# Two blocks' modulations move from the recurrence to the first phase; the recurrence's filler becomes the gates alone, read in halves of rows

## The chip, the core and the metric

The kernel runs on one core of a Trainium2 chip. The metric is the device time of one execution in microseconds (us), as the median of several runs. One further execution was taken by the hardware profiler; all rows below are from that one.

The engines are named as in the profile: PE is TensorE's matmuls, PEld its weight loads, DVE is VectorE, ACT is ScalarE, POOL is GpSimd, and SP is SyncE, which here only issues DMA transfers. Every engine runs its own instructions in the order in which they were written, and waits at one whose inputs or buffers are not ready.

## The reference

Two transformer-like blocks run one after the other on a sequence of 512 latent tokens (width 1024), with 256 context tokens beside them. The parts that matter here are these, of the first block:

```
s_lat = silu(c);  s_ctx = silu(c_ctx)
mod   = s_lat @ w_ada + b_ada             # six rows of 1024: shift, scale, gate, twice
p_l   = modulate(x, norm1_g, mod[0], mod[1]) @ w_in        # p_c: the same of the context
pool_l, q_l, k_l, v_l, rw_l, gate_l = split(p_l)
att   = differential attention of q_l over the keys of context and latent
rwo   = rwkv: a recurrence over all tokens, in both directions, of rw_c and then rw_l
mix   = sum over n of sigmoid(gate_l[n]) * (branch[n] @ w_br[n]),  then @ w_out
x     = x + mod[2] * mix
x     = x + mod[5] * moe(modulate(x, norm2_g, mod[3], mod[4]))
```

The second block has two layers, each with modulations of its own (`ada_w_0`, `ada_w_1`: 1024 x 6144, times the silu of a second pair of vectors). `mod[0]` and `mod[1]` are needed before anything else. `mod[2]` to `mod[5]` are needed only where the branches are merged, and the second block's only behind the experts. The 24 tiles of `gate_l` (three branches of eight 128-wide tiles) are likewise needed only in the merge.

## The kernel before

Almost all values are float32. A product of a weight and an activation is made of three matmuls of rounded halves (`gemm_k`: high by high, high by low, low by high), and a weight tile is read from DRAM, rounded by ACT (`wgh<-wg`, a CAST) and its remainder formed by DVE (`wgl<-wg,wgh`).

`head1` computes `mod[0]`, `mod[1]` and the normed inputs. Then come two stages that this text is about.

**The first phase** (`phase1`, line 738) weaves four streams: `rwkv_inputs` (projections `gp<-..,ww..` and what the recurrence needs, among it the products `lora`, `dg`, `kss`), `attend` (projections `wa`, then scores `S`, transposes `pt`, value products `o`), `pools_gates` (the pooling branch `wo`, `py`) and `rwkv_blocks` (a small inversion on DVE). Their ranks are 0, 0, 2, 0.

**The recurrence** (`rwkv`, line 1384) weaves two lanes of steps (`rwkv_step`: `pc`, `pw`, `py`, rank 0), two streams of units (`rwkv_unit`: `tkp`, `m`, `pg`, `pT`, `pZ`, `pZt`, `pR`, `pf`, ending in the tile `Zl`; rank 1) and fillers of rank 2. There are 24 units, one for each of four channel groups and six blocks of tokens, and a step waits for the `Zl` of its unit. At most three units are ahead of the steps (`AHEAD`). Most matmuls of units and steps stream 128 or 256 columns.

The fillers of the recurrence are two. The first is `ada_steps`: `mod[2]` to `mod[5]` (`w_ada_b`, 64 pieces of 256 KB) and the first of the second block's modulations (`ada_w0`, 96 pieces). Each piece is one float32 matmul `ada<-wada,adas` with 512 columns and 32 output rows, and four of them in a row go to four different quarters of the output:

```
for j in range(4):
    self.mm(p[32 * j:32 * j + 32], z[:, g + j, ...], W[j], start=..., stop=..., skip_group_check=True)
```

The profile shows each of these as two records, so 160 pieces are 320 records. The second filler is `gates`: for each of the 24 tiles, the projection of the latent tokens (`gp<-h1l_hi,wgh` and its two fellows, 512 columns each), then a tanh (`gt`) and a write to DRAM. Its weights come through a `Feed`, which reads `kc` of the eight row blocks at a time (128 KB a read for `kc=2`), `ahead` reads before they are rounded; a read can start only when the buffer `ahead` places back has been rounded.

Which stream comes next is settled when the program is written, by `weave` and an estimate of when things will be ready (`Clock`):

```
low = 2 if self.clock.active() < self.LOW else 0
x = min(ready, key=lambda x: (x[1] < low, *x[1:3])) if ready else min(S, key=lambda x: x[:3])
```

A filler of rank 2 is thus placed where no stream of lower rank is ready by that estimate, and also where the estimate finds TensorE little used. Nothing is decided at run time. SP's reads stand in one queue in the order of writing, those of the next stage behind those of the stage before.

Of the kernel before, what the change touches and what calls it, by code (L numbers as in the profile page):

```python
# [417 lines left out]
class Builder:  # L418
# [288 lines left out]
    def phase1(self, es):  # L707


        nc, D, tc = self.nc, self.D, self.tc  # L710
        dt = lambda n, sh: tc.dram_tile(sh, FT, name=n)
        self.d_ar = dt("rw_ar", [4, 2, 128, 6, 2, 128])
        self.d_bk = dt("rw_bk", [4, 2, 128, 6, 2, 128])
        self.d_inv = dt("rw_inv", [4, 6, 2, 128, 2, 2, 32])
        self.d_vt = dt("rw_vt", [4, 128, 6, 128])
        self.d_bg = dt("rw_bg", [4, 128, 2, NL])
        self.d_q = dt("at_q", [4, 128, NL])
        self.d_k = dt("at_k", [4, 128, NT])
        self.d_v = dt("at_v", [4, 128, 6, 128])
        self.d_g = dt("gates", [3, 8, 128, NL])  # L720
        self.d_br = [dt(n, [4, 128, NL]) for n in ("pooled", "attended", "rw_out")]
        self.fac = self.pool(es, "keep1").tile([128, 4, 2, 6, 2], FT, name="fac")
        with ExitStack() as e:
            hl = self.pool(e, "h1l")
            self.h1l = [hl.tile([128, 8, NL], FR, name=n) for n in ("h1l_hi", "h1l_lo")]
            with ExitStack() as e2:
                hc = self.pool(e2, "h1c")
                self.h1c = [hc.tile([128, 8, NCX], FR, name=n) for n in ("h1c_hi", "h1c_lo")]
                with ExitStack() as e3:
                    self.banks = dict(g=4, s=4)  # L730
                    self.psp = self.pool(e3, "psh", 1, space=PSUM)
                    self.head1(e3)
                self.banks = dict(g=3, f=2, s=2, h=1)
                self.psp = self.pool(e2, "ps0", 1, space=PSUM)
                self.lat, self.both = [(*self.h1l, 0, NL)], [(*self.h1c, 0, NCX), (*self.h1l, 0, NL)]
                with ExitStack() as e3, ExitStack() as e4:
                    self.todo = []
                    self.weave(*zip(self.RANKS, (self.rwkv_inputs(e3), self.attend(), self.pools_gates(e4), self.rwkv_blocks())))
            self.banks = dict(s=6, g=1, h=1)
            self.psp = self.pool(e, "ps2", 1, space=PSUM)  # L740
            self.rwkv(e)

# [31 lines left out]
    def pools_gates(self, es):  # L774
        with ExitStack() as e:
            yield from self.pool_mixer(e)
        if self.GATES_A:
            yield from self.gates(es, range(self.GATES_A), "h", 3, 4, side="right")

    def gates(self, es, which, tag, ahead, kc, **k):  # L780

        nc = self.nc
        ring = self.pool(es, "gring", **k)
        wp = self.pool(es, "gate", **k)
        at = [(i // 8, i % 8) for i in which]
        feed = self.feed_in(ring, "g", [f"g{b}{n}" for b, n in at], ahead, kc)
        for b, n in at:
            (o,) = yield from self.proj(feed, self.lat, tag)
            t = wp.tile([128, NL], FT, name="gt", tag="gt")
            nc.scalar.activation(t, o, AF.Tanh, scale=0.5)  # L790
            nc.scalar.dma_start(self.d_g[b, n], t)
            yield self.after(t)
# [591 lines left out]
    def rwkv(self, es):  # L1384
        nc = self.nc
        pp = self.pool(es, "rwc", 1)
        up = self.pool(es, "rwu", 1)
        made, done = [0], [0]
        self.levels = pp.tile([128, 3, 2, 128], FT, name="levels")
        nc.scalar.dma_start(self.levels, self.D["levels"])  # L1390

        todo = [(c + q, n) for c in range(0, 4, self.LANES) for n in range(6) for q in range(self.LANES)]
        ch = {}

        def units(q):
            while todo:
                while made[0] - done[0] >= self.AHEAD:
                    yield self.later()
                if todo:
                    c, n = todo.pop(0)  # L1400
                    made[0] += 1
                    P = {}
                    yield from self.rwkv_unit(c, n, up, q, P)
                    ch[c, n] = P

        def steps(q):
            for c in range(q, 4, self.LANES):
                if c == q:
                    while not ch:
                        yield self.later()  # L1410
                V = up.tile([128, 6, 2, 2, 64], FR, name="V", tag=f"V{q}")
                vl = V[:, :, :, 1].bitcast(FT)
                nc.sync.dma_start(vl, self.d_vt[c].rearrange("p j (h v) -> p j h v", h=2))
                nc.scalar.copy(V[:, :, :, 0], vl)
                nc.gpsimd.tensor_sub(V[:, :, :, 1], vl, V[:, :, :, 0].bitcast(FT))
                st = dict(V=V, q=q, y=up.tile([128, 4, 128], FT, name="ysb", tag=f"ysb{q}"), seen=set(), S=None)
                for n in range(6):
                    while (c, n) not in ch:
                        yield self.later()
                    yield from self.rwkv_step(c, n, ch.pop((c, n)), st, up)  # L1420
                    done[0] += 1
                self.dump(f"ysb{c}", st["y"])
                yield from self.rwkv_out(c, st["y"], pp)

        gens = [(0, steps(q)) for q in range(self.LANES)] + [(1, units(q)) for q in range(self.UNITS)]
        self.weave(*gens, (2, self.ada_steps(self.pool(es, "adaw"), self.ada_jobs())),
                   (2, self.gates(es, range(self.GATES_A, 24), "g", 1, 2)))
        nc.vector.tensor_add(self.mod1[:, 16:], self.mod1[:, 16:], self.v("b_ada", 16, 32))


    def rwkv_unit(self, c, n, up, q, P):
# [1504 lines left out]
```

## Time and profile before

| | |
|---|---|
| median of 3 runs | 4063.65 us (4059.62 to 4070.69) |
| the profiled execution's own time | 4066.27 us |
| its span, first to last instruction | 4064.5 us |
| PE busy | 3701.7 us (91%) |
| DVE, ACT busy | 2373.9 us (58%), 1647.9 us (41%) |
| mean granted TensorE clock | 0.937 of full |

In this execution the first phase's matmuls begin at 57 us, attention's scores at 366 us, the recurrence's first fillers at 649 us, and its last step's at about 1310 us; then come the merge, the experts and the second block. Busy shares are means over all of that. A granted clock of 1.00 is TensorE's upper level of 2.4 GHz and 0.50 its lower of 1.2 GHz; a stretch between them held both in turn.

### The profile page before, as it was taken

Reading aid. Unit: us, or ns where it says so; the run is one execution under the profiler, and the core shown is the slowest. Engines: PE = TensorE matmul, PEld = TensorE weight load, DVE = VectorE, ACT = ScalarE, POOL = GpSimd, SP = SyncE. Lnnn points to the kernel's source line nnn. Section 1 sums busy time; section 2 is a strip of 40 time slices with the busy share of each in tenths; the row PEclk is TensorE's granted clock in tenths of the full one; section 3 lists DMA queues with packets and bytes.
Section 4 is the critical chain, followed back from the end, with each engine's and each line's share of the span. In section 5 each row is a group of like instructions: output and inputs, shape, how many; then the busy total and the mean of one; then the engine's idle time right before and its main releaser. Section 6 shows DMA issues by size and latency. Waiting matters only on the chain.

```text
span 4064.5 us, 51183 instructions
## 1 busy us (share of the span) xinstructions
PE 3701.7 (91%) x18740; PEld 2861.0 (70%) x18740; DVE 2373.9 (58%) x4428; ACT 1647.9 (41%) x2933; POOL 525.3 (13%) x750
## 2 busy tenths in 40 slices
PE   8999777898997789999988999899999999999998
PEld 4776445676777667666655887587888877667886
DVE  5578766666665558888874566545323335445444
ACT  3333323443443237666653554223313324434342
POOL 0222122222221211111110000110100100000010
PEclk9999758999997889999999999999999999999999
DMA  5233113434341729989964334411221220012332
GB/s 186 96 94 107 69 59 117 130 117 139 118 135 65 273 103 368 333 333 337 330 226 163 127 114 145 140 34 55 63 65 60 84 62 27 13 42 83 99 94 88
DMA packets 220098, 538.00 MB, mean 132 GB/s; under 512 B 42051, under 2 KB 76516, under 8 KB 193349
## 3 DMA queue, kind: packets, MB, share of 16 engines
q1 hardware_dynamic: 179152, 461.38, 33.5%
q10 hardware_dynamic: 36852, 61.79, 4.3%
q0 software_dynamic: 3840, 11.54, 0.9%
q8 instruction: 149, 2.44, 0.3%
q14 instruction: 105, 0.85, 0.1%
HBM read 486.38 MB, written 48.24 MB: 132 GB/s over the span
## 4 chain that ended last, share of the span: by engine, by line
PE 61%; DVE 10%; DMA 5%; ACT 4%; issue 3%; POOL 1%; SPq 0%; another core or an unknown queue 0%; ACTq 0%; DVEq 0%; POOLq 0%
PE gp L355 34%; PE eg L355 5%; PE ed L355 3%; DVE el L355 2%; PE S L355 2%; DMA wg<-w_in_a 2%; PE vp L355 1%; PE eT L355 1%; PE o L355 1%; PE ada L355 1%; PE cp L355 1%; PE pc L355 1%; PE fk L355 1%; ACT eh L355 1%; DVE Mt L355 1%
## 5 line engine op out<-in xcount | busy, mean ns | idle before, releaser
L355 ACT CAST wh<-wr 128x512 fp32r<-128x512 f32 (+5 forms) x306 | 199.8, 676 | 602.4 <-PE gp L355 538.0
L355 PE MATMUL gp<-h_hi,wh 128*128 128x512 f32 (+1 forms) x1128 | 401.5, 359 | 6.7 <-ACT h_hi L355 4.0
L355 DVE TENSOR_TENSOR el<-ew,eh 128x1024 fp32r<-128x1024 f32 x284 | 354.2, 1273 | 58.6 <-ACT eh L355 56.9
L355 PE MATMUL gp<-h_lo,wh 128*128 128x512 f32 (+1 forms) x1128 | 386.2, 357 | 0.6 <-DVE h_lo L355 0.3
L355 DVE TENSOR_TENSOR wl<-wr,wh 128x512 fp32r<-128x512 f32 (+5 forms) x306 | 227.9, 764 | 248.3 <-ACT wh L355 247.7
L355 PE MATMUL gp<-h_hi,wl 128*128 128x512 f32 (+1 forms) x1128 | 343.3, 356 | 0.0
L355 ACT CAST eh<-ew 128x1024 fp32r<-128x1024 f32 x288 | 292.9, 1048 | 17.1 <-PE ec L355 11.1
L355 PEld LDWEIGHTS gp<-h_hi,wh 128*128 128x128 f32 x1128 | 211.9, 189 | 57.7 <-ACT h_hi L355 8.9
L355 PEld LDWEIGHTS gp<-h_lo,wh 128*128 128x128 f32 x1128 | 213.0, 189 | 34.8 <-DVE h_lo L355 3.1
L355 PEld LDWEIGHTS gp<-h_hi,wl 128*128 128x128 f32 x1128 | 189.8, 190 | 16.7 <-DVE wl L355 0.3
L355 PE MATMUL gp<-z_hi,wh 128*128 128x512 f32 (+1 forms) x528 | 187.8, 356 | 0.0
L355 PE MATMUL eg<-el,xg 128*128 128x512 f32 x384 | 161.7, 421 | 27.9 <-DVE el L355 27.7
L355 PE MATMUL gp<-z_lo,wh 128*128 128x512 f32 (+1 forms) x528 | 179.2, 354 | 0.0
L355 PE MATMUL eg<-eh,xg 128*128 128x512 f32 x384 | 176.3, 459 | 0.1
L355 PE MATMUL ada<-wada,adas 128*32 128x512 f32 (+1 forms) x576 | 141.1, 642 | 25.4 <-DMA wada<-ada_w 12.4
L355 PE MATMUL gp<-z_hi,wl 128*128 128x512 f32 (+1 forms) x528 | 158.8, 355 | 0.0
L355 POOL MEMSET cvb<- 128x1 f32 x170 | 9.6, 98 | 1062.7 <-DVE fg L355 691.6
L355 PE MATMUL gp<-h_lo,wih 128*128 128x256 f32 (+1 forms) x384 | 132.2, 344 | 0.0
L355 PE MATMUL gp<-h_hi,wih 128*128 128x256 f32 (+1 forms) x384 | 129.1, 357 | 0.0
L355 PEld LDWEIGHTS eg<-el,xg 128*128 128x128 f32 x384 | 72.4, 189 | 70.2 <-DVE el L355 51.5
L355 PE MATMUL eg<-ew,xw 128*128 128x512 f32 x256 | 120.2, 592 | 0.0
L355 PEld LDWEIGHTS gp<-z_hi,wh 128*128 128x128 f32 x528 | 99.1, 188 | 22.7
(853 smaller groups left out, 9631.8 us busy)
## 6 DMA issues: line engine op xcount, KB each, us to landing
ew<-w_exp SPq DMA_DIRECT2D x192, 1024.0 KB, 6.9
wada<-ada_w SPq DMA_DIRECT2D x192, 256.0 KB, 3.6
wr<-ffn_up SPq DMA_DIRECT2D x176, 256.0 KB, 2.7
wada<-w_ada_b SPq DMA_DIRECT2D x64, 256.0 KB, 3.5
wg<-w_in_a SPq DMA_DIRECT2D x96, 128.0 KB, 2.3
wi<-w_in SPq DMA_DIRECT2D x48, 256.0 KB, 2.8
wr<-ffn_dn SPq DMA_DIRECT2D x32, 384.0 KB, 3.1
wr<-ffn_dn SPq DMA_DIRECT2D x32, 320.0 KB, 3.2
```

Of the source, the lines that this page charges most:

```text
L355: return f(*a, **k)
```

## The change

The modulations' stream is appended to the pooling branch's stream of the first phase, at rank 2, with nine buffers in place of five, and is no longer woven into the recurrence. The gates are then the recurrence's only filler; they are read four row blocks at a time and two reads ahead, in place of two and one. The recurrence's PSUM banks are divided anew: seven for units and steps, one for the gates.

```
@@ phase1
-            self.banks = dict(s=6, g=1, h=1)
+            self.banks = dict(s=7, g=1)
             self.psp = self.pool(e, "ps2", 1, space=PSUM)
             self.rwkv(e)
@@ pools_gates
+        yield from self.ada_steps(self.pool(es, "adaw", side="right"), self.ada_jobs(), 9)
+        self.nc.vector.tensor_add(self.mod1[:, 16:], self.mod1[:, 16:], self.v("b_ada", 16, 32))
@@ rwkv
-        self.weave(*gens, (2, self.ada_steps(self.pool(es, "adaw"), self.ada_jobs())),
-                   (2, self.gates(es, range(self.GATES_A, 24), "g", 1, 2)))
-        nc.vector.tensor_add(self.mod1[:, 16:], self.mod1[:, 16:], self.v("b_ada", 16, 32))
+        self.weave(*gens, (2, self.gates(es, range(self.GATES_A, 24), "g", 2, 4)))
```

Three places show what this does to the order. The first is PE in the attention half of the first phase, near the end of a chunk's inputs for the recurrence. Before:

```order
L355 MATMUL pt<-const_58,P 128x128 x4
L355 MATMUL lora<-alt,a_369 128x512
L355 MATMUL pt<-const_58,P 128x128 x2
L355 MATMUL lora<-alt,a_369 128x256
L355 MATMUL S<-kx,q 128x384 x2
L355 MATMUL dg<-BK,AR 128x128 x8
```

And a like place of the changed kernel:

```order
L355 MATMUL lora<-alt,a_369 128x512
L355 MATMUL pt<-const_58,P 128x128 x4
L355 MATMUL ada<-wada,adas 32x512 x4
L355 MATMUL lora<-alt,a_369 128x256
L355 MATMUL pt<-const_58,P 128x128 x2
L355 MATMUL S<-kx,q 128x384 x2
L355 MATMUL ada<-wada,adas 32x512 x13
L355 MATMUL dg<-AR,BK 128x128 x8
L355 MATMUL ada<-wada,adas 32x512 x3
```

All 160 pieces now stand in this half, between scores, transposes and the recurrence's inputs. Here thirteen stand in one run; over the whole half there are 54 runs of one to thirteen (19 single pieces, 11 pairs, 7 of three, 8 of four, 9 longer). Before, they stood in 51 runs of one to four, all in the recurrence.

The second place is SP in the first phase, where `ww` are weights of the recurrence's inputs and `q`, `kx`, `V` are attention's operands. Before:

```order
L355 DMA ww<-w_in_a 128x512
L355 DMA wg<-w_in_a 128x256
L355 DMA wada<-w_ada_b 128x512 x4
L355 DMA wg<-w_in_a 128x256
L355 DMA wada<-w_ada_b 128x512
L355 DMA wg<-w_in_a 128x256
L355 DMA V<-at_v 128x768
L355 DMA ww<-w_in_a 128x512
```

Of the changed kernel:

```order
L355 DMA ww<-w_in_a 128x512
L355 DMA wada<-w_ada_b 128x512 x17
L355 DMA ww<-w_in_a 128x512
L355 DMA wada<-w_ada_b 128x512 x7
L355 DMA q<-at_q 128x512
L355 DMA kx<-at_k 128x768
L355 DMA V<-at_v 128x768
L355 DMA ww<-w_in_a 128x512
```

The later reads of `ww`, `q`, `kx` and `V` now stand behind reads of modulation weights, each of which waits for one of nine buffers.

The third place is PE in the recurrence, just ahead of the `pf` of the sixteenth of the 24 units. Before:

```order
L355 MATMUL pT<-G,TZ 128x128 x4
L355 MATMUL gp<-h1l_hi,wgh 128x512
L355 MATMUL gp<-h1l_lo,wgh 128x512
L355 MATMUL gp<-h1l_hi,wgl 128x512
L355 MATMUL ada<-wada,adas 32x512
L355 MATMUL pZt<-const_58,T 128x128 x4
L355 MATMUL pR<-T,Ah 128x128
L355 MATMUL pR<-T,Al 128x128
```

Of the changed kernel:

```order
L355 MATMUL pT<-G,TZ 128x128 x4
L355 MATMUL pZ<-TZ,identr 128x512
L355 MATMUL pZ<-TZ,G 128x128 x4
L355 MATMUL pZt<-const_58,T 128x128 x4
L355 MATMUL pR<-T,Ah 128x128
L355 MATMUL pR<-T,Al 128x128
```

The filler is gone from there. In the changed order 23 of the 24 gates stand ahead of the ninth unit's `pf` and the last ahead of the tenth's; before, about twelve stood ahead of the ninth's, and the last ahead of the 23rd's.

## Rows read from the trace of the kernel before

**Rows 1.** Windows, core 0: stretch; busy us (count) per engine; clock; DMA share, GB/s.

```profile
355.00:645.00 290.00, 222.39 (x757) 134.40 (x756) 214.01 (x524) 95.59 (x233) 46.47 (x51) 0.71 0.20 65
645.00:913.00 268.00, 242.02 (x1535) 189.22 (x1536) 165.84 (x296) 111.89 (x235) 64.69 (x91) 0.95 0.43 133
913.00:1262.00 349.00, 317.89 (x2080) 254.34 (x2078) 223.88 (x438) 143.13 (x295) 80.63 (x95) 0.94 0.39 123
1262.00:1312.00 50.00, 39.77 (x210) 36.40 (x208) 24.74 (x60) 12.99 (x25) 2.54 (x2) 0.65 0.18 64
```

**Rows 2.** Windows, tile `Zl`, DVE alone: one instruction for each finished unit.

```profile
645.00:913.00 268.00, 11.36 (x9) 0.95 0.43 133
```

**Rows 3.** Tile view of `gt`: the tanh that ends each gate, with first and last start.

```profile
L355 ACT ACTIVATE gt<-gp x24: 584/591/602, 658.5 to 1261.6; 128x512 f32<-128x512 f32 x24
```

**Rows 4.** Windows, tile `wgl`: a third of the gates' matmuls; PE, PEld, DVE.

```profile
645.00:913.00 268.00, 39.14 (x94) 18.75 (x94) 23.31 (x47) 0.95 0.43 133
913.00:1262.00 349.00, 40.44 (x98) 19.40 (x98) 21.28 (x47) 0.94 0.39 123
```

**Rows 5.** Windows, tile `wada`: the modulations' matmuls; PE, PEld, ACT.

```profile
645.00:913.00 268.00, 26.02 (x144) 4.48 (x144) 0.59 (x1) 0.95 0.43 133
913.00:1262.00 349.00, 34.63 (x192) 5.73 (x192) 0.59 (x1) 0.94 0.39 123
```

**Rows 6.** Timeline of PE: start, length, what; a gate's quarter, three runs of modulations.

```profile
1198.30 1.91 PE L355 MATMUL ada<-wada,adas 128*32 128x512 f32 x2
...
1209.64 1.05 PE L355 MATMUL ada<-wada,adas 128*32 128x512 f32 x2
...
1254.67 1.07 PE L355 MATMUL ada<-wada,adas 128*32 128x512 f32 x8
...
1256.92 0.50 PE L355 MATMUL gp<-h1l_hi,wgh 128*128 128x512 f32 x1
...
1258.42 0.60 PE L355 MATMUL tkp<-const,BKl 128*128 128x128 f32 x4
```

**Rows 7.** The chain of waits, 645 to 1262 us: shares by line.

```profile
by line: PE gp L355 10.9%; DMA wg<-w_in_a 10.6%; PE pc L355 5.2%; issue 4.5%; PE m L355 4.2%; PE ada L355 4.1%; DVE Mt L355 4.1%; PE pT L355 3.8%; DVE wgl L355 2.9%; PE pZ L355 2.7%; PE pg L355 2.5%; PE pw L355 2.4%; ACT wgh L355 2.2%; PE p
```

**Rows 8.** Groups of ACT, 645 to 1262 us: busy, mean ns, idle before.

```profile
L355 ACT CAST wgh<-wg 128x256 fp32r<-128x256 f32 x94 | 38.2, 406 | 119.1 <-DMA wg<-w_in_a 76.4 <-PE gp L355 34.4 <-PE pT L355 4.1
```

**Rows 9.** Windows where units and steps ran with little or no filler (columns as Rows 1).

```profile
1021.00:1038.00 17.00, 17.00 (x73) 16.08 (x73) 5.13 (x8) 5.71 (x11) 6.43 (x6) 0.51 0.14 45
...
1262.00:1273.00 11.00, 9.51 (x66) 7.25 (x64) 8.40 (x17) 5.04 (x11) 0.00 (x0) 1.00 0.58 216
1273.00:1287.00 14.00, 13.86 (x63) 13.41 (x63) 4.70 (x8) 3.64 (x8) 0.00 (x0) 0.51 0.00 1
1287.00:1290.00 3.00, 2.17 (x19) 2.01 (x19) 0.85 (x2) 0.96 (x2) 0.00 (x0) 1.00 0.00 0
1290.00:1312.00 22.00, 14.23 (x67) 13.73 (x66) 10.80 (x34) 3.36 (x6) 2.54 (x2) 0.50 0.11 37
```

**Rows 10.** Timeline of PE: the same product at either clock.

```profile
1287.22 0.27 PE L355 MATMUL pc<-Rs,Zl 128*128 128x128 f32 x1
1287.33 0.28 PE L355 MATMUL pc<-Rs,Zh 128*128 128x128 f32 x1
...
1305.62 0.41 PE L355 MATMUL pc<-Rs,Zl 128*128 128x128 f32 x1
1305.83 0.41 PE L355 MATMUL pc<-Rs,Zh 128*128 128x128 f32 x1
```

**Rows 11.** Windows of the attention half, two of its half-clock stretches.

```profile
433.00:484.00 51.00, 35.52 (x103) 22.35 (x103) 41.39 (x89) 13.12 (x30) 12.26 (x12) 0.50 0.20 75
...
580.00:638.00 58.00, 34.76 (x86) 19.30 (x87) 42.44 (x101) 13.44 (x35) 10.31 (x6) 0.50 0.14 48
```

**Rows 12.** DMA issues: operation and count, KB each, median us from issue to landing.

```profile
wada<-w_ada_b SPq DMA_DIRECT2D x64, 256.0 KB, 3.5
```

## The prediction

> **What bounds the kernel now.** I read the page first: PE is busy 91% of the span and no other engine comes near, so the question is what PE does where work is taken away and where it arrives. Both places are in the first 1312 us; behind them PE's order differs only at some 300 positions of the second block, where its own last modulations stand a little earlier, which I price at nothing: the same matmuls run there. The windows by stage come next [rows 1]. In the attention half of the first phase (355 to 645) PE is busy 222.4 of 290 us at a granted clock of 0.71. In the recurrence (645 to 1312, 667 us) it is busy 242.0 of 268, 317.9 of 349 and 39.8 of 50 us. There are 24 units; nine are done by 913 us [rows 2], and the split at 913 is chosen because in the changed order 23 gates stand ahead of the ninth unit's end.
>
> The recurrence looks bound by PE with filler on top. Then I asked what the filler does for the clock. The last gate ends at 1262 [rows 3]. Until 1273 the clock holds at 1.00; then it falls to the lower level (0.51 and 0.50) and stays there but for 3 us, with PE busy 13.9 of 14 us in the first half-clock stretch [rows 9]. Much the same happened at 1021 to 1038, where units alone ran before gates came back: 17.00 of 17.00 us busy at 0.51. So a PE full of the units' small matmuls did not hold the upper level, nor regain it, in the stretches seen. At the lower level the same product starts every 0.21 us in place of every 0.11 [rows 10].
>
> **The gates' and modulations' price.** A quarter gate (six matmuls) takes 1258.42 - 1256.92 = 1.50 us [rows 6], so a gate takes 6.0 and all 96 quarters 144. Of the 192 `wgl` matmuls 94 lie before 913 and 98 behind [rows 4]: 70.5 and 73.5 us of gates. The modulations hold PE for 26.0 and 34.6 us [rows 5]. What is left is units and steps: 242.0 - 70.5 - 26.0 = 145.5 us before 913, and 317.9 - 73.5 - 34.6 + 39.8 = 249.6 behind.
>
> **Recurrence, first nine units.** Now 145.5 + 23 x 6.0 = 283.5 us of PE work, where there were 242.0. PE was idle 268 - 242 = 26 us. Filler is denser and its weights come earlier, so I keep 16 of idle: 299.5 us, **+31** (idle 6: +21; idle 26: +41). The earlier weights are a real gain here. The chain of waits goes through reads of gate weights for 10.6% of 617 us [rows 7], and ACT sat 76.4 us before casts of them [rows 8], with the units' copies queued behind each cast. But PE was mostly working in those waits; what can come back is no more than its idle time, and 10 of 26 us are already credited.
>
> **Recurrence, the other fifteen.** No filler is left after the tenth unit. In the half-clock stretches of [rows 9] PE was busy 17.0 + 13.9 + 14.2 = 45.1 us, which the upper level would do in 0.11/0.21 = 0.524 of that, 21.5 us less. So the work is 249.6 - 21.5 + 6.0 (the last gate) = 234 us at the upper level, against the 399 us that this part took (913 to 1312). What counts is the share of time at the upper level. From 1273 to 1312 it was 3 of 39 us, 8%; with the 11 us right behind the last gate, 14 of 50, 28%. I take 15%, since a steady flow of steps has more wide products than the end of the stage, and no gates. The rate is then 0.15 + 0.85 x 0.524 = 0.595, the work takes 393 us, and with 5% idle (0.0 of 17 us at 1021, 10.2 of 50 at the very end) 414: **+15**. At 28% it is 375 (-24), at 8% 438 (+39). The modulations that left and the idle time that shrank are thus paid back by the clock.
>
> Here the Trainium skill speaks the other way. Its page "TensorE: Matmul & The Clock Gate", section "What's actually happening", says that the throttled state is the default and that "activity releases the throttle": a busy PE should regain 2.4 GHz. The trace disagrees where it can be asked: 17.00 of 17.00 us busy, granted 0.51 [rows 9]. By the rule this part would be the first rival below; I go by the row.
>
> **Attention half of the first phase.** 160 pieces arrive. A run of one piece holds PE 1.05 us and a run of four 1.07 at the upper level, and one piece 1.91 at the lower [rows 6]; a run thus costs one slot for each four begun. The changed order has 67 slots (45 runs of up to four, nine longer ones with 22). That is 71 us at the upper level or 128 at the lower. A mean of 0.71 [rows 1] is 42% upper and 58% lower, which gives 104 us, against 67.6 us of idle PE: 36 us too much if nothing else moves. Against this, 58% of 290 us is 168 us at the lower level; in the two stretches shown PE was busy 35.5 + 34.8 of 109 us [rows 11], so some 108 us of work runs at half speed and would lose 51 us if the pieces held the upper level. Scores and transposes are links between DVE and ACT steps, and DVE is busy 214 of 290 us, so I let at most 20 of the 51 shorten the stage. Ends -20 and +36; I take the middle, **+8**.
>
> Here new waits arise. PE can wait at a piece for its read, with scores and `dg` queued behind it; and SP's reads of `q`, `kx`, `V` and `ww` stand behind reads that wait for one of nine buffers. One landing takes 3.5 us [rows 12]. Bytes are no matter: 42 MB more in 290 us is 145 GB/s on top of 65, with the DMA engines at 0.20 [rows 1]. I price these waits at nothing in the sum, because other streams' matmuls stand in front of most of them, and at a whole landing each in a rival.
>
> **At no price.** The casts of gate weights are halved in number and doubled in width; ACT and DVE have room, at 112 and 166 of 268 us [rows 1]. A seventh bank for units and steps: no row names a bank, and a loss is excluded, since the gates kept theirs. The bias addition is one DVE instruction, needed only in the merge.
>
> **Sum.** +31 + 15 + 8 = +54 us, on the profiled execution's 4066.27 (span 4064.5 and 1.8 around it): 4120. The median of the runs is 2.6 below that execution, so **4118 us**. Its own ends, -20 - 24 + 21 = -23 and 36 + 39 + 41 = +116, give 4041 to 4180.
>
> **Rivals.**
>
> *The clock holds in the unfilled part* (the other side: faster). Place: the fifteen units behind the last gate. At the upper level throughout, with the idle share of the end, 39.8 of 50 busy, they take 234/0.80 = 293 us, -106; with +31 and +8 the sum is -67, **3997**. It decides from a share of about 39% at the upper level: then the part takes 348 us, 51 less, and the whole 12 less. For it speaks that 1262 to 1273 was at 1.00 without gates; against it, everything from 1273 on. 15%.
>
> *The late gate weights were lost time after all.* If the 10.6% of the chain, 65 us, came back whole, 4118 falls to **4053**, which is no difference. Against it: PE's idle time from 645 to 1262 was 57 us in all, more than half of it in the part that has no gates now. 10%.
>
> *The reads hold up attention.* SP's order has some 12 places where a read of `ww`, `q` or `V` follows reads of modulations. A landing at each is 42 us; with the 36 left over, the half grows by 78 in place of 8: **4188**. For it: the run of thirteen pieces has only nine buffers. Against it: other streams' matmuls stand in between. 18%.
>
> **How the numbers follow.** My forecast has 55%; 2% are for things not thought of. A measurement here tells about 0.3%, 12 us, from no change. Faster: the first rival and the 2%, 0.17. Same: the late weights and the low end of the forecast, 0.12. Slower: 0.71. For 8 in 10 the range takes the forecast's ends, the late weights and the stalled reads, and leaves out the clock that holds: 4040 to 4190.
>
> **What would show it.** Right: gates' tanhs all done by about the ninth `Zl`; behind that a granted clock near 0.6, PE almost without idle, and units no quicker than before (some 26 us each); modulations between scores from about 360 us; few waits of ACT for gate weights. Wrong: a clock of 0.8 or more behind the last gate, units of 20 us there, or an attention half shorter by more than 20 us or longer by more than 36.

## The result, and the profile after

The changed kernel takes **4098.28 us**, the median of 5 runs (4092.32 to 4104.02); the kernel before took 4059.62 beside it (5 runs, 4054.33 to 4070.69). The ratio is 1.0091, with a 95% interval of 1.0075 to 1.0106: slower by 0.9%, 39 us. Forecast were 4118, in a range of 4040 to 4190. The profiled execution of the changed kernel took 4104.02 us, with a span of 4102.2 and a mean granted clock of 0.922 (before 0.937).

From the page of the changed kernel, PE's line of busy time and the line of the granted clock in 40 slices of the span (103 us each, tenths of full speed):

```profile
PE 3768.9 (92%) x18740; PEld 2936.3 (72%) x18740; DVE 2362.3 (58%) x4380; ACT 1642.9 (40%) x2885; POOL 529.4 (13%) x750
PEclk9999987997566789999999999999999999999999
```

The same line of the kernel before:

```profile
PEclk9999758999997889999999999999999999999999
```

PE does the same 18,740 matmuls, and is busy 67 us longer than before: nothing was added, so the same work ran slower. The clock lines say where: slices 11 to 14, from about 1026 to 1436 us, hold 5, 6, 6 and 7, and before 9, 9, 7 and 8. (Slices 5 and 6, in the attention half, have risen from 7 and 5 to 9 and 8.)

The windows of the changed kernel answer to [rows 1] (stretch; busy us and count of PE, PEld, DVE, ACT, POOL; clock; DMA share, GB/s). The bounds are the same events as before: the end of attention, the ninth unit, the last unit.

```profile
355.00:661.00 306.00, 271.14 (x1091) 133.54 (x1090) 218.25 (x533) 98.18 (x238) 47.24 (x52) 0.88 0.57 189
661.00:942.00 281.00, 268.07 (x1641) 230.59 (x1641) 172.34 (x285) 124.47 (x239) 67.05 (x90) 0.97 0.30 93
942.00:958.00 16.00, 15.36 (x78) 12.94 (x79) 11.61 (x25) 4.66 (x9) 3.50 (x7) 0.68 0.15 42
958.00:1342.00 384.00, 328.49 (x1738) 305.20 (x1737) 215.36 (x420) 131.66 (x254) 80.14 (x90) 0.63 0.12 36
```

The attention half has grown by 16 us in this execution (306 for 290), the first nine units by 13 (281 for 268). The other fifteen take 16 + 384 = 400 us; in the trace of before, their last `Zl` starts 391 us behind the ninth's, here 401. That is +16 +13 +10 = +39 us, and behind the last step the two traces take the same (2752 us, 2754 before), so the whole loss lies here. The split is that of one pair of executions, both some 6 us above their medians; e9 below has a second one of the changed kernel. Behind the last gate PE is busy 328.5 of 384 us at 0.63.

The tile views of the changed kernel: the gates' tanh, which answers to [rows 3], and the copies `os` of attention's value products, the last of which ends its half (count: shortest, median, longest ns; first and last start).

```profile
L355 ACT ACTIVATE gt<-gp x24: 587/592/609, 674.1 to 956.5; 128x512 f32<-128x512 f32 x24
...
L355 ACT COPY os<-o x4: 582/586/587, 456.6 to 657.4; 128x512 f32<-128x512 f32 x4
```

All gates are done by 956.5, 16 us behind the ninth unit, as the order had it. The last `os` starts at 657; before, at 641.

Windows of the tiles `wgl` (recurrence) and `wada` (attention half) of the changed kernel answer to [rows 4, 5] (PE and PEld, then DVE or ACT):

```profile
661.00:942.00 281.00, 76.05 (x188) 36.40 (x188) 37.22 (x46) 0.97 0.30 93
942.00:1342.00 400.00, 1.84 (x4) 1.03 (x4) 0.00 (x0) 0.63 0.12 36
...
355.00:661.00 306.00, 79.24 (x318) 13.82 (x318) 1.19 (x2) 0.88 0.57 189
```

The groups of the changed kernel: in the recurrence, 661 to 1342, ACT's casts of gate weights, which answer to [rows 8]; in the attention half the modulations and the scores (busy, mean ns; idle before, by releaser).

```profile
L355 ACT CAST wgh<-wg 128x512 fp32r<-128x512 f32 x46 | 28.5, 620 | 64.9 <-PE gp L355 53.3 <-DMA ARl<-rw_ar 11.6
...
L355 PE MATMUL ada<-wada,adas 128*32 128x512 f32 x302 | 77.2, 666 | 4.9 <-DMA wada<-ada_w 3.4 <-DMA wada<-w_ada_b 1.5
L355 PE MATMUL S<-kx,q 64*128 64x384 f32 x128 | 57.5, 569 | 10.6 <-ACT P L355 7.6 <-DMA kx<-at_k 3.0
```

ACT's 76.4 us of waiting for gate weights are gone, and the kernel is slower all the same. PE waited 4.9 us for modulation weights and 3.0 for a read of keys, 8 us in all: the reads did not hold up attention.

### The profile page after: what moved, and what is told of

Read it like the earlier page. It is cut to its first block, busy times and chain, and to the rows that moved or that the text cites. A ratio compares the mean times of both kernels' runs of the same rounds, so it can differ in the third digit from the quotient of the medians.

```text
span 4102.2 us, 50939 instructions
## 1 busy us (share of the span) xinstructions
PE 3768.9 (92%) x18740; PEld 2936.3 (72%) x18740; DVE 2362.3 (58%) x4380; ACT 1642.9 (40%) x2885; POOL 529.4 (13%) x750
## 4 chain that ended last, share of the span: by engine, by line
PE 74%; DVE 13%; DMA 4%; ACT 4%; issue 3%; POOL 2%; SPq 0%; ACTq 0%; another core or an unknown queue 0%; DVEq 0%; POOLq 0%
PE gp L355 39%; PE eg L355 5%; PE ed L355 3%; PE S L355 3%; PE ada L355 2%; DVE el L355 2%; PE pT L355 2%; PE o L355 1%; PE pc L355 1%; PE vp L355 1%; PE m L355 1%; PE eT L355 1%; PE cp L355 1%; PE pZ L355 1%; PE pg L355 1%
## 5 line engine op out<-in xcount | busy, mean ns | idle before, releaser
L355 PE MATMUL ada<-wada,adas 128*32 128x512 f32 (+1 forms) x576 | 161.3, 655 | 28.7 <-DMA wada<-ada_w 13.4
```

Of the source, the lines that this page charges most:

```text
L355: return f(*a, **k)
```

## Experiments

Theory C, the clock, is that the loss comes from the units without filler, because units and steps alone are granted the lower level most of the time. Its rivals: the modulations in the attention half, reads of weights, or the recurrence's chain itself, whatever PE's clock. Every edit is to the changed kernel. "Before" is the kernel before on the same chip: 4055.21 beside e1 to e4, 4055.42 beside e5 to e8, 4056.37 beside e9 to e11. A ratio is made from all runs of both kernels, so it need not be the quotient of the two medians. e3 and e4, of one run each, stand in their own paragraphs.

| run | last gate's tanh, us | time, us (runs) | ratio to before, 95% |
|---|---|---|---|
| changed, again (e9) | 944 | 4092.08 (4) | 1.0091 (1.0073 to 1.0109) |
| quarters, two ahead (e5) | 1063 | 4060.39 (10) | 1.0005 (0.9989 to 1.0020) |
| quarters, one ahead (e1) | 1168 | 4049.70 (10) | 0.9985 (0.9967 to 1.0004) |
| spread, quarters, one ahead (e6) | 1254 | 4042.99 (10) | 0.9969 (0.9954 to 0.9983) |
| spread, quarters, four ahead (e7) | 1259 | 4032.44 (4) | 0.9937 (0.9916 to 0.9959) |
| spread, halves, one step (e8) | 1261 | 4034.61 (4) | 0.9947 (0.9929 to 0.9965) |
| spread, halves, two steps (e2) | 1231 | 4014.34 (7) | 0.9922 (0.9898 to 0.9946) |
| the same again (e10) | 1246 | 4034.34 (5) | 0.9941 (0.9916 to 0.9966) |
| spread, halves, three steps (e11) | 1224 | 4029.62 (10) | 0.9939 (0.9916 to 0.9961) |

**The move alone (e1).** The modulations stay in the first phase; the gates are read as before.

```
-   self.gates(es, range(self.GATES_A, 24), "g", 2, 4)
+   self.gates(es, range(self.GATES_A, 24), "g", 1, 2)
```

> One edit of the two: the modulations stand in the first phase as in the change, but the gates are still read two row blocks at a time, one read ahead. In its order the gates reach to the twentieth unit in place of the tenth. Theory C (the clock: units without 512-column filler run at the lower TensorE clock, and that pays back the modulations' work): the granted clock of the recurrence is again above 0.85, the stage loses most of the modulations' 61 us, and with the 16 us that attention grew by the whole takes 4015 to 4045 us. Rival R (the loss is the modulations' removal as filler, not the halves): the clock behind the tenth unit is about 0.65 and the whole takes 4090 to 4110 us, like the changed kernel.

4049.70 us, ratio 0.9985 (0.9967 to 1.0004): no difference from before, and 49 us below the changed kernel. The clock theory's range was missed by 5 us, and the rival's is out. So the move by itself loses nothing, and shows no gain; with the new reading of the gates on top, 49 us are lost. With one quarter ahead, the gates last until 1168 us; with two halves ahead, all 24 stand ahead of the tenth unit. That the estimate then sees weights ready sooner, and so places a gate wherever it may, is argued from the code, not shown. The windows of this run (columns as in [rows 1]; from the ninth unit to the last gate, then to the last unit):

```profile
886.00:1170.00 284.00, 254.59 (x1577) 214.16 (x1576) 189.16 (x370) 121.17 (x251) 70.89 (x83) 0.90 0.22 67
1170.00:1290.00 120.00, 99.73 (x563) 92.48 (x563) 66.88 (x139) 38.36 (x75) 16.11 (x14) 0.69 0.10 34
```

With gates the clock is 0.90, without them 0.69. The other half, the new reading with the modulations left in the recurrence, was not tried.

**Gates spread over the units (e2, e10).** The gates' stream hands back to the planner three times for each gate (at its two halves and at its tanh), so `i` counts thirds of gates: at most one gate more is placed for each step done, two steps ahead.

```
+   def spread(g):
+       for i, t in enumerate(g):
+           while i >= 3 * (done[0] + 2):
+               yield self.later()
+           yield t
...
-   (2, self.gates(es, range(self.GATES_A, 24), "g", 2, 4))
+   (2, spread(self.gates(es, range(self.GATES_A, 24), "g", 2, 4)))
```

> The changed kernel, with one rule more: a gate is placed only when the steps done are no more than two behind its number, so that the 24 gates are spread over the 24 units, one for each. Theory C: the clock of the recurrence is about 0.9 to its end, ACT does not wait for gate weights, and the stage falls from about 691 us to 590 to 625: 4000 to 4035 us. Rival L (the unfilled part is bound by hand-offs between engines, whatever the clock): the same work in another order, 4085 to 4105 us.

> The gates released one for each step, two steps ahead, once more and beside the changed kernel on one chip. If its lead is its own: 4005 to 4030, 70 to 90 us below the changed kernel. If the first measurement was a lucky one: 4030 to 4045, as the paced quarters and the lead of one.

4014.34, and 4034.34 in the second measurement, 58 us below the changed kernel beside it; both measurements beat both kernels (0.9922 and 0.9941). The work and the reads are those of the changed kernel; the order is not, and in it units and steps too stand at other places than there, not only the gates. As expected of the clock theory, the second part's clock is high in the windows of the first of the two runs:

```profile
649.00:890.00 241.00, 216.78 (x1332) 185.96 (x1333) 154.56 (x263) 105.15 (x203) 67.70 (x90) 0.89 0.22 69
890.00:1240.00 350.00, 319.24 (x2052) 282.28 (x2051) 233.82 (x434) 150.54 (x291) 81.85 (x95) 0.91 0.20 65
1240.00:1265.00 25.00, 16.96 (x105) 16.31 (x104) 16.10 (x44) 6.14 (x12) 2.53 (x2) 0.69 0.12 44
```

Nine units 40 us shorter than in the changed kernel, for fewer gates are among them; the other fifteen take 364 us for 401 (from the ninth `Zl` to the last), with some thirteen gates more. This profiled execution, of 4009.28 us, is the fastest of the twelve of both measurements, which lie between 4009 and 4040; that of e10 is the median of its five, and its windows are these:

```profile
655.00:898.00 243.00, 215.09 (x1338) 184.84 (x1339) 155.79 (x271) 105.99 (x205) 67.27 (x89) 0.90 0.22 68
898.00:1246.00 348.00, 317.90 (x1997) 280.05 (x1996) 231.55 (x428) 146.93 (x285) 82.70 (x96) 0.89 0.19 59
1246.00:1276.00 30.00, 27.36 (x134) 26.10 (x132) 13.54 (x36) 7.94 (x15) 0.00 (x0) 0.58 0.24 88
```

There the fifteen take 377 us by the same bounds, still 24 less than in the changed kernel with thirteen gates more among them. By what e10 was expected to tell, the first measurement was a lucky one.

**Gates twice (e3).** 24 more gates, whose results are written over the first: 144 us of useless PE work.

```
-   range(self.GATES_A, 24)
+   [*range(24), *range(24)]
```

> The changed kernel, computing all 24 gates twice (the second time for nothing), so that filler lasts to about the twentieth unit; 24 x 6.0 = 144 us of TensorE work at the upper clock is added. Theory C: that work is nearly paid for by the clock it keeps up, 4090 to 4140 us, with a clock of at least 0.9 up to the twentieth unit. Rivals W and L (work in the in-order queue, or hand-offs, set the pace): 4220 to 4245 us.

4135.25 us (one run), 37 above the changed kernel, in the clock theory's range and 85 us below that of its rivals: the clock theory is shown here. The same ten units, the tenth to the nineteenth, can be compared: first the changed kernel's windows (all engines, then tile `Zl` on DVE), then those of this run (the same, then tile `wgl`).

```profile
942.00:1204.00 262.00, 233.50 (x1206) 216.18 (x1206) 151.67 (x293) 92.85 (x178) 64.77 (x79) 0.62 0.14 44
...
942.00:1204.00 262.00, 12.59 (x10) 0.62 0.14 44
```

```profile
937.00:1243.00 306.00, 289.89 (x1782) 250.35 (x1782) 186.14 (x346) 134.04 (x253) 65.61 (x79) 0.96 0.28 88
...
937.00:1243.00 306.00, 12.12 (x10) 0.96 0.28 88
...
937.00:1243.00 306.00, 78.29 (x192) 37.50 (x192) 32.97 (x47) 0.96 0.28 88
```

192 `wgl` matmuls are 24 gates, 144 us by the price of [rows 6]. What is left for ten units is 289.9 - 144 = 146 us, where without gates they hold PE for 233.5. A clock of 0.62 is 24% at the upper level, so a rate of 0.24 + 0.76 x 0.524 = 0.64, and 233.5 x 0.64 = 149: the clock accounts for nearly the whole 88 us. A count without that price agrees: timed in the two traces from each matmul's start to the next one's start (or its own end, where that is sooner), units and steps hold PE for 230 us in the changed kernel and 145 here. The two orders differ in the places of units and steps as well, but e4 below, whose order differs from the changed kernel's at about as many places (some 1080 of 2916 in each, gates left out), differs from it by 17 us of PE time over all fifteen units, and not by 84 over ten. What it is about the gates that keeps the clock up was not tried. Idle time shrank by 12 us (28.5 to 16.1). So 144 us of work lengthen the stretch by 44.

**No modulations (e4).** Their matmuls and reads are left out; zeros stand in their places.

```
-   yield from self.ada_steps(self.pool(es, "adaw", side="right"), self.ada_jobs(), 9)
+   for _, _, *out in self.ada_jobs():
+       for t in out:
+           if t is not None:
+               self.nc.gpsimd.memset(t, 0.0)
```

> The changed kernel without the modulations of the first phase: neither read nor computed (zeros in their place). Theory A (the pieces in TensorE's queue cost the attention half its 16 us): attention ends about 16 us earlier, at its clock of before, 0.71, and the recurrence is as in the changed kernel: 4075 to 4090 us. Rival B (the pieces' clock gave back what they took, and the 16 us are from the reads' place on SP's queue or from chance in the order): the stage stays as long without them, 4095 to 4105 us.

4059.79 us (one run), below either range. The attention half ends at 637 us, 20 sooner than in the changed kernel's profile, with its clock at 0.71 as in [rows 1]; that is the modulations' price in this pair of profiles (12 us against the mean of eleven, e9 below). The other 22 us were not expected: the last fifteen units take 378 us for 400, though the same work is in them. The recurrence's order comes out otherwise at over a thousand places of PE's order, and its clock behind the last gate is 0.67 for 0.63:

```profile
942.00:1301.00 359.00, 308.37 (x1731) 284.81 (x1731) 214.46 (x418) 130.59 (x254) 81.63 (x90) 0.67 0.12 37
```

With the 18.4 us before it, PE is busy 326.7 us over these units, 17 less than in the changed kernel. Why that order holds the clock better stays open. It does suggest that an unfilled stretch can take some 20 us more or less by its order alone.

**Quarters, two ahead (e5).**

```
-   "g", 2, 4)
+   "g", 2, 2)
```

> The changed kernel with its gates read two row blocks at a time, but two reads ahead. In its order the gates reach to the fifteenth unit: between the tenth of the changed kernel and the twentieth of the run with only the modulations moved. Theory C (what counts is how many units are left without filler, because they run at the lower clock): a time between those two, 4055 to 4085 us, and a granted clock of about 0.95 up to the fifteenth unit and 0.6 to 0.7 behind it. Rival LR (late gate weights are the larger cost, and two reads ahead heal them): 4045 us or less.

4060.39, in the clock theory's range. The last gate is done at 1063, between the changed kernel's and e1's, and so is the time. ACT waits 1.6 us for gate weights here and 40.5 in e1 (the next fence), and yet e1 has the lower median, by 11 us (the intervals just overlap): what the ended wait may give is paid back where the filler ends earlier.

**Spread, with late or early reads (e6, e7).** As e2, but the gates are read in quarters, one ahead or four ahead; with quarters the stream hands back five times for each gate, so five for each step.

```
+   while i >= 5 * (done[0] + 2):
...
-   "g", 2, 4)
+   "g", 1, 2)    # e6
+   "g", 4, 2)    # e7
```

> Gates spread one to a unit by the same rule as in the paced run, but read as in the kernel before: two row blocks at a time, one read ahead. It takes the early reads out of the paced run (4014 us) and leaves its spreading. Theory C (the spreading is the gain): 4010 to 4030 us, with ACT's waits for gate weights back at 50 us or more and mostly beside the path. Rival LR (the early reads are the gain): 4040 to 4060 us, about the run with only the modulations moved.

> Gates spread one to a unit, read two row blocks at a time and four reads ahead: as early as in the paced run, in smaller bursts on TensorE. Theory C, with bursts of no account: 4005 to 4020 us. Rival G (a burst of twelve matmuls ahead of a step is felt, and small ones hold the clock more evenly): 3985 to 4000 us.

4042.99 and 4032.44. For e6 the rival was right: with late reads the spread gates are 7 us below e1 by the medians, and the two intervals overlap, so no gain is shown. For e7 neither range holds it. Their casts of gate weights (groups of ACT, 650 to 1300 us), one fence each for e1, e6 and e7:

```profile
L355 ACT CAST wgh<-wg 128x256 fp32r<-128x256 f32 x94 | 38.1, 405 | 65.9 <-DMA wg<-w_in_a 40.5 <-PE gp L355 23.4 <-PE m L355 0.9
```

```profile
L355 ACT CAST wgh<-wg 128x256 fp32r<-128x256 f32 x94 | 38.1, 406 | 84.0 <-DMA wg<-w_in_a 51.8 <-PE gp L355 27.4 <-DMA gates<-gt 2.0
```

```profile
L355 ACT CAST wgh<-wg 128x256 fp32r<-128x256 f32 x94 | 37.9, 405 | 67.1 <-PE gp L355 59.7 <-issue 2.3 <-DMA ARl<-rw_ar 1.0
```

51.8 us of ACT's waiting for reads are gone in e7, and the time is 10.6 us less. The two intervals (0.9954 to 0.9983, 0.9916 to 0.9959) overlap by little, so early reads are probably worth some 10 us once the filler is spread.

**Leads of one and three steps (e8, e11).** As e2, with another lead.

```
+   while i >= 3 * (done[0] + 1):    # e8
+   while i >= 3 * (done[0] + 3):    # e11
```

> The paced run with the gates held one step further back (one in place of two ahead of the steps done), so that filler is left for the last units too. Theory C: the stretch behind the last gate shrinks by one unit, 5 to 10 us less than the paced run: 4004 to 4012 us. Rival: the first units have one gate less each and run at the lower clock in exchange, 4014 us or more.

> Gates released one for each step, three steps ahead in place of two; three gates more stand early, and the last is done about two units sooner. Clock theory: the part without filler grows by one to two units, 5 to 10 us over the lead of two, so 4015 to 4030. Rival (the lead gives the reads time, and the lead of one lost 20 us for the lack of it): another gain, 3995 to 4010.

4034.61 and 4029.62. e8 missed the clock theory's range and fell into its rival's; e11 fell into the clock theory's. Neither counts for much, for both expectations were reckoned from e2's 4014. Taken with e10's 4034.34, leads of one to three are not told apart: the 20 us by which e8 came out behind e2 were the luck of e2's first measurement, so there is no loss for its rival to explain, and e11 did not come out behind the lead of two, as the clock theory had it.

**The changed kernel again (e9).**

> The changed kernel once more, for the part of its loss that lies in the first phase. Its order there is that of the four variants whose attention half ended at 643, 645, 649 and 653 us, and its own ended at 657. If what the 160 pieces cost there varies from execution to execution (theory V), this profile ends the half at another time, 643 to 655, and the time is 4090 to 4105 as before. If it is the kernel's own (theory O: code or data placed otherwise by the different recurrence), the half ends at 656 to 658 again. In both, the ninth unit comes 280 to 285 us behind the half's end and the last 400 behind the ninth, at a clock of 0.63.

4092.08 us, and theory V was right. The windows of this execution, by the same events as the changed kernel's first:

```profile
355.00:648.00 293.00, 255.39 (x1107) 126.75 (x1106) 219.63 (x537) 99.60 (x240) 47.33 (x52) 0.94 0.59 198
648.00:928.00 280.00, 268.53 (x1641) 231.70 (x1641) 170.78 (x283) 124.42 (x239) 66.53 (x90) 0.97 0.30 94
928.00:1328.00 400.00, 345.94 (x1820) 319.40 (x1821) 226.15 (x444) 136.37 (x264) 82.44 (x97) 0.62 0.11 36
```

The same order ended its attention half at 644 us here, 13 sooner than in the first profile, at a clock of 0.94 for 0.88; then come 280 us for nine units and 400 for fifteen, as there. So the 16 us of the attention half are one execution's. This order of the first phase stands in eleven profiles, e4 apart; the last `os` starts from 643 to 657, 649 on average, against 641 in the one profile of before. Against that profile the three parts are +3, +12 and +9 here, 24 in all, where the medians differ by 36: the traced execution of before, 4066.27 us, was itself some 10 us above the median of 4056.37 beside e9. In which part is not known, so each part's difference may be off by as much.

## Why the prediction was right

It said slower, by 54 us against the profiled execution, with most of it in the recurrence; measured were 39 between the medians. Direction and mechanism held. Of the three terms, one was mis-sized, one was near by errors that cancelled, and one was right as a mean. Against the first profile they are off by 18 and 5 us too much and 8 too little, and these too cancel in part.

**First nine units: +31 predicted, +13 measured, below the lower bound of +21.** This is the term that was mis-sized. Idle time was not the error: 12.9 us, where 16 were kept. The error is the units' own work, which I carried over unchanged at 145.5 us. By the same price, 188 `wgl` matmuls are 141 us of gates, and 268.1 - 141 = 127 is left for units and steps: 18 us less. Part of that is the price: timed as under e3, from start to start, the gates of before took 75.8 us and not 70.5, and units and steps 141.5 us before and 128.4 after, 13 less. Of these, 4 are fewer matmuls, 1077 for 1109 (1535 - 3 x 94 - 144). The clock, which I let be, is worth 3: 28 of their matmuls start at the lower level, for 49 before, each some 100 ns longer there. The last 6 are matmuls at the upper level, which took 117 ns each for 123 before; why was not settled.

**The other fifteen: +15 predicted, +10 measured.** Each number in it was off. A clock of 0.63 means 26% at the upper level, near the bound of 28% and not the 15% that I took. The prediction's 399 us ran to the end of the last step, and so does this window of the changed kernel:

```profile
942.00:1352.00 410.00, 350.39 (x1843) 324.32 (x1843) 230.44 (x454) 137.06 (x265) 83.63 (x97) 0.63 0.12 35
```

PE's work is 350.4 us busy at a rate of 0.26 + 0.74 x 0.524 = 0.648, or 227 at the upper level, not 234. The 234 had set right the 45 us of the stretches shown; by the clock of 0.94 in [rows 1] some 42 us up to 1262 were at the lower level, of which it had counted 17. Idle time is 59.6 of 410 us, 15%, not 5%. PE's two largest waits (total us, times, longest), first from 942 to 1342 us of the changed kernel, then from 913 to 1302 us of the kernel before:

```profile
PE ytp L355 <- DVE ysb L355: 20.5, 3, 8.5
PE pc L355 <- DVE Rs L355: 11.7, 5, 4.7
...
PE ytp L355 <- DVE ysb L355: 11.0, 3, 5.0
PE pc L355 <- DVE Rs L355: 7.0, 8, 1.7
```

Together 227 / 0.648 / 0.855 = 410, where I had 414. With the 5% of idle time that I took, this clock would have given 369 us, 30 less than before and beyond my bound of -24; idle time, more than half of it these two waits for DVE (32 us, 18 before), which I had not priced, kept the part at a loss.

The rule of the Trainium skill that was weighed there ("TensorE: Matmul & The Clock Gate", section "What's actually happening", activity releases the throttle) can be asked again. From 1156 to 1193 us of the changed kernel, with units and steps alone:

```profile
1156.00:1193.00 37.00, 35.97 (x156) 33.09 (x155) 19.00 (x33) 12.24 (x25) 5.78 (x9) 0.50 0.06 19
```

PE is busy 36.0 of 37 us and granted 0.50 throughout. The trace disagrees with the rule as far as busy time is the activity meant.

**Attention half: +8 predicted, +16 in this profile, +8 over eleven (each against the one profile of before).** I had PE's pieces at 104 us and let 20 come back. They held it for 79 us, since the clock of the half went from 0.71 to 0.88, and the other work shrank from 222 to 271 - 79 = 192: 30 came back. Against these two gains, the pieces did not fill all of PE's 67.6 us of idle time, as the sum had it, but 33 of them: 79 - 30 - 33 = 16.

**The rivals.** *The clock holds*: no; it needed 39% at the upper level, and there were 26%. *Late gate weights were lost time*: ACT's waits for them went from 76.4 us to nothing and nothing was gained as long as the gates ended early (e5); spread, some 10 us of it come back (e6 against e7), not 65. *The reads hold up attention*: no, 8 us of PE's waiting.

**What the prediction did not see** is which edit did it. It took the gates' end at the tenth unit as given by the change as a whole, and named the modulations that left as what laid the part bare. e1 shows that the modulations can leave without loss. It is with the deeper reads that the planner spent the gates early; that its estimate then found them always ready is read from the code, and not shown.

## What to carry to other kernels

Where a stretch runs at the lower clock unless filler lies among its matmuls, filler is worth more than its own time, and its place counts: 24 gates with early reads, spread over all units, gave medians of 4014 to 4035 us, the same gates in one heap 4092 to 4098, and 144 us of useless gates cost only 37. A wait that is taken away may change what an offline planner writes much more than it saves: look at the order for where the filler runs out, and release it by progress, not by readiness. A stage's work must be priced anew at the clock that the change gives it, and its idle time too: two waits for DVE grew here from 18 to 32 us where the filler had left.

## What the runs showed of the hardware

The same fifteen units and their steps in two orders, each with only the end of the filler at its start, ran at 0.67 and 0.63 behind it and took 378 and 400 us (e4, one run, against the changed kernel). The same instructions of the first phase ended between 643 and 657 us in eleven profiles, and two of them are of the very same kernel (644 and 657). From 942 to 1204 us of the changed kernel, matmuls of units and steps took 125 ns on average, start to start, where the granted clock was 1.00, and 223 ns where it was 0.50; among gates, in e3 from 937 to 1243 us, 117 and 194. What the filler changed was above all how many were granted which: 817 of 1194 the lower level there, 54 of 1205 in e3.
